# Up blocks of a gated FFN formed by token instead of by feature, and turned by DMA

## The chip, the cores and the metric

The kernel runs on one core of one Trainium2 chip. The metric is device time in microseconds of one execution, the median over runs. The engines are TensorE (PE; its weight loads are listed as PEld), VectorE (DVE), ScalarE (ACT), GpSimd (POOL) and SyncE (SP), whose queue issues nearly all DMAs here. SBUF is the memory that engines and DMAs work from; PSUM takes what TensorE forms.

## The reference

One decoder layer on 256 tokens of width 2048, in float32: retention and a gated linear recurrence side by side, a gated merge, attention over 256 memory tokens, a convolved gated FFN, and a last norm. The change is in the FFN:

```
def causal_dwconv(x, w, bias):
...
def conv_gated_ffn(hn, w_up, conv_w, conv_b, w_down):
    up = causal_dwconv(hn @ w_up, conv_w, conv_b)
    gate, val = jnp.split(up, 2, axis=-1)
    return (jax.nn.silu(gate) * val) @ w_down
...
    hn = rmsnorm(h, norm_ffn_w[l])
    h = h + conv_gated_ffn(hn, ffn_w_up[l], ffn_conv_w[l], ffn_conv_b[l], ffn_w_down[l])
    return rmsnorm(h, final_norm_w)
```

`w_up` is 2048 x 11264 (5632 gate features, then 5632 value features). The convolution has three taps over tokens, one set per feature. `w_down` is 5632 x 2048.

## The kernel before

All weights are streamed once from HBM, in one order fixed beforehand (`weight_plan`), in chunks of four k tiles: 4 x 128 rows of 512 columns, 1 MB. A block is 512 columns over all rows, so four chunks for 2048 rows. `prefetch` issues each chunk's load on SP's queue into one of three raw buffers and splits it in halves of two k tiles: `hi` is the weight rounded to the float32r that TensorE multiplies (L248, on ACT), `lo` the remainder (L249, on DVE). There are six buffers of each, three chunks' worth; two chunks are split ahead of the one in use. The activations are split the same way, in pairs of k tiles: a tile `s` holds hi in columns 0 to 255 (tokens) and lo in columns 256 to 511. Each product is formed as hi\*hi + hi\*lo + lo\*hi.

There are two forms of a block.

By feature (`gemm_t`, L309): 128x128 of the weights is held stationary, tokens stream. With `hi` held, one matmul of 512 columns multiplies both halves of `s`; with `lo` held, one of 256 multiplies the hi half. The result has features on partitions, in two accumulators of 128x2x512, each with two sums that have still to be added: `joined` copies one (L388, ACT) and adds the other (L389, DVE).

By token (`gemm_n`, L322 to L324): the activations are held stationary, 128 tokens of one k tile, and 512 weight columns stream; three matmuls for each k tile and each half of the tokens. The result has tokens on partitions, in one accumulator.

The norms' factor for each token is applied behind the product. In the by-feature form it varies along the free axis, so DVE multiplies by a copy spread over all partitions (`scaled`, L528). In the by-token form it is one number for each partition.

`by_dma` turns 256 tokens x 512 features around. ACT copies the two 16-bit halves of each float32 into two planes (L367); two DMA transposes on SP's queue, one for each half of the tokens, turn the planes (L369); one chunk later (`later(1, join)`) ACT puts the halves together again (L378) and hands the result on. It is used for the merge and for the two residuals, `residual` (L800 is the add, L815 the squares for the norm), whose results are needed by feature next.

The FFN runs in three parts of four, four and three pairs of blocks (`FF_PARTS`). A pair is a gate block and a value block of `w_up`, each by feature: `conv_up` takes the accumulators as they come, applies `scaled`, and does the convolution, one tap on ACT (L916) and two on DVE (L918). Then the gating: tanh on ACT (L985), two operations on DVE (L986, L987), and the split into `hid` (L399, L400). After a part's up blocks come its four down blocks, by token, with `hid` held stationary and the result added to the rows of the residual stream (`down`, L929). The last part's last down block also does the final norm.

The order of instructions on each engine is set by a scheduler that goes by the order in the program and by priorities; `tc.high_priority(URGENT)` moves a step ahead. Accumulators come from a pool of three, the large SBUF tiles (`big`) from a pool of 27.

Of the kernel before, what the change touches and what calls it, by code (L numbers as in the profile page):

```python
# [13 lines left out]
AF = mybir.ActivationFunctionType  # L14
ALU = mybir.AluOpType
AX = mybir.AxisListType

P = 128
D = 2048
S = 256  # L20
NT = D // P
# [5 lines left out]
FF = 5632  # L27
NF = FF // P
BW = 512
# [6 lines left out]
URGENT = 5  # L36
# [79 lines left out]
def hybrid_layer(  # L116
# [16 lines left out]
    act, dve, pe, pool, sp = nc.scalar, nc.vector, nc.tensor, nc.gpsimd, nc.sync  # L133
# [11 lines left out]
    def nm(s):  # L145
        count[0] += 1
        return f"{s}_{count[0]}"

    def big(shape, dt=F32, s="b"):
        return bp.tile(shape, dt, tag="big", name=nm(s))  # L150

    def tmp(s="t"):
        return tp.tile([P, 2, S], F32, tag="tmp", name=nm(s))
# [19 lines left out]
    pf = cp.tile([P, 4, NF2], F32, name="pf")  # L173
# [85 lines left out]
    def later(n, fn):  # L259

        pending.append((step[0] + n + 1, fn))
# [18 lines left out]
    def ended(steps):  # L280

        for a in steps:
            pass
        return a
# [31 lines left out]
    def gemm_t(*args):  # L316
        return ended(steps_t(*args))
# [8 lines left out]
    def steps_n(w, row, st, nk, col):  # L326

        a = acc()
        for k0, n, parts in chunks(nk, w, row, col):
            for tt in range(2):  # L330
                for kk in range(n):
                    k = k0 + kk
                    hi, lo = (t[:, kk % KH, :] for t in parts[kk // KH])
                    products_n(a[:, tt, :], st[k // 2][:, k % 2, :], hi, lo, tt, k == 0, k == nk - 1)
            yield a

    def gemm_n(*args):
        return ended(steps_n(*args))
# [21 lines left out]
    def by_dma(rows, then):  # L360


        planes = big([P, 2, 2, BW], U16, s="pl")
        turned_ = big([P, 2, 4, S], U16, s="pt")
        words = rows.bitcast(U16).rearrange("p t (n h) -> p h t n", h=2)
        for h in range(2):
            act.copy(planes[:, :, h, :], words[:, h])  # L367
        for tt in range(2):
            sp.dma_start_transpose(  # L369
                out=turned_.rearrange("p h f s -> p (h f) s")[:, :, tt * P : (tt + 1) * P],  # L370
                in_=planes[:, tt].rearrange("p h n -> p (h n)"),
            )

        def join():
            f = big([P, 4, S], s="f")
            halves_ = f.bitcast(U16).rearrange("p f (s h) -> p h f s", h=2)
            for h in range(2):
                act.copy(halves_[:, h], turned_[:, h])  # L378
            then(f)

        later(1, join)

    def joined(a, s="j"):

        c = tmp("c")
        o = tmp(s)
        with tc.high_priority(URGENT):
            act.copy(c, a[:, :, S:BW])  # L388
            dve.tensor_tensor(out=o, in0=a[:, :, 0:S], in1=c, op=ALU.add)  # L389
        return o  # L390

    def split_pair(src, scale=None):

        t = big([P, 2, BW], F32R, s="s")
        if scale is None:
            act.copy(t[:, :, 0:S], src)
            dve.tensor_tensor(out=t[:, :, S:BW], in0=src, in1=t[:, :, 0:S].bitcast(F32), op=ALU.subtract)
        else:
            act.mul(t[:, :, 0:S], src, scale)  # L399
            dve.scalar_tensor_tensor(  # L400
                out=t[:, :, S:BW], in0=src, scalar=scale, in1=t[:, :, 0:S].bitcast(F32),
                op0=ALU.mult, op1=ALU.subtract,
            )
        return t
# [32 lines left out]
    def p_cw(i, t):  # L437
        return pa[:, 16 + i * 16 + t : 17 + i * 16 + t]
# [32 lines left out]
    def rstd_rows(ss):  # L471

        var = sp_.tile([P, 2], F32, tag="var", name=nm("var"))
        dve.tensor_reduce(out=var, in_=ss, axis=AX.X, op=ALU.add)
        return rsqrt_small(var, 2, 1.0 / D, EPS)
# [50 lines left out]
    def scaled(a, s):  # L526
        z = joined(a, s)
        dve.tensor_tensor(out=z, in0=z, in1=rsb2, op=ALU.mult)  # L528
        return z
# [115 lines left out]
    for g in range(2):  # L645
        dec = big([P, 4, S], s="dec")
        vs, turned = [], []
        for b, o in enumerate((O_Q, O_K)):
            a = [joined(t, "q") for t in gemm_t("w_in", 0, xs, NT, o + g * BW)] if g + b else qjoin
            if b == 1:  # L650
                sp.dma_start(
                    out=dec,
# [10 lines left out]
        for b in range(2):  # L663
            a = gemm_n("w_in", 0, xs, NT, O_G + g * 1024 + b * BW)
            t = big([P, 2, BW], s="gate")
# [70 lines left out]
    for b in range(4):  # L736
# [4 lines left out]
        for pr, a in enumerate(gemm_t("w_in", 0, xs, NT, O_XR + b * BW)):  # L741
            z = scaled(a, "xz")
            for j in range(2):
                t = 4 * b + 2 * pr + j
                y = xr[:, 2 * pr + j, :]
                act.activation(y, z[:, j, :], AF.Identity, scale=p_cw(3, t), bias=p_cb(t))
                for s in range(1, 4):
                    dve.scalar_tensor_tensor(  # L748
                        out=y[:, s:S], in0=z[:, j, 0 : S - s], scalar=p_cw(3 - s, t), in1=y[:, s:S],
                        op0=ALU.mult, op1=ALU.add,  # L750
                    )
        gl = big([P, 4, S], s="gl")
        for pr, a in enumerate(gemm_t("w_in", 0, xs, NT, O_YR + b * BW)):
            y = scaled(a, "yz")
            y2, th = tmp("y2"), tmp("yt")
# [5 lines left out]
                out=gl[:, 2 * pr : 2 * pr + 2, :], in0=th, scalar=1.0, in1=y, op0=ALU.add, op1=ALU.mult  # L761
# [21 lines left out]
    for b in range(4):  # L783
        m = gated(O_GA, "w_proj_ret", ret, b, big([P, 2, BW], s="m"))
        dve.tensor_add(m, m, mb[b])
        by_dma(m, turn_merged)
# [6 lines left out]
    def residual(w, st, out, wcol, steps=None):  # L793

        ss = sums()
        for b in range(4):
            if steps:
                steps(b)
            h = hrow[b]
            dve.tensor_add(h, h, gemm_n(w, 0, st, NT, b * BW))  # L800
            squares(h, ss, b)
            by_dma(hrow[b], lambda f, b=b: turn(f, b, out, wcol))
        return ss
# [70 lines left out]
    for b in range(XH):  # L874
        ks = []
        for a in gemm_t("xa_w_k", 0, ms, NT, b * BW):
            z = joined(a, "kz")
# [26 lines left out]
    h2s = []  # L904
    ss2 = residual("xa_w_o", osp, h2s, p_ffn)
    rs2 = rstd_rows(ss2)
    later(1, spread_tokens(rs2))


    def conv_up(c0, b, dst):  # L910
        for pr, a in enumerate(gemm_t("ffn_w_up", 0, h2s, NT, c0 + b * BW)):
            z = scaled(a, "uz")
            for j in range(2):
                t = c0 // P + 4 * b + 2 * pr + j
                y = dst[:, 2 * pr + j, :]
                act.activation(y, z[:, j, :], AF.Identity, scale=pf[:, 2, t : t + 1], bias=pf[:, 3, t : t + 1])  # L916
                for s in range(1, 3):
                    dve.scalar_tensor_tensor(  # L918
                        out=y[:, s:S], in0=z[:, j, 0 : S - s], scalar=pf[:, 2 - s, t : t + 1], in1=y[:, s:S],
                        op0=ALU.mult, op1=ALU.add,  # L920
                    )

    def down(b0, hid, b, final):

# [49 lines left out]
    b0 = 0  # L974
    for part, nb_ in enumerate(FF_PARTS):
        final = part == len(FF_PARTS) - 1
        hid = []
        for b in range(b0, b0 + nb_):
            gt, vl = big([P, 4, S], s="fg"), big([P, 4, S], s="fv")
            conv_up(0, b, gt)  # L980
            conv_up(FF, b, vl)
            for pr in range(2):
                cs = slice(2 * pr, 2 * pr + 2)
                th, o = tmp("ft"), tmp("fo")
                act.activation(th, gt[:, cs, :], AF.Tanh, scale=0.5)  # L985
                dve.scalar_tensor_tensor(out=o, in0=th, scalar=1.0, in1=gt[:, cs, :], op0=ALU.add, op1=ALU.mult)  # L986
                dve.tensor_tensor(out=o, in0=o, in1=vl[:, cs, :], op=ALU.mult)  # L987
                hid.append(split_pair(o, 0.5))
        if final:
            wfin = []  # L990
            for i in range(2):
                t = big([P, 2, BW], s="wf")
                sp.dma_start(
                    out=t.rearrange("p a n -> p (a n)"),
                    in_=final_norm_w[i * 1024 : (i + 1) * 1024].partition_broadcast(P),
                )
                wfin.append(t)
        for b in range(4):
            down(b0, hid, b, final)
        b0 += nb_  # L1000
# [33 lines left out]
```

## Time and profile before

| | |
|---|---|
| median of 3 runs | 2039.36 us (2038.9 to 2040.87) |
| the profiled execution | 2038.96 us, its span 2037.2 |
| mean granted clock of TensorE | 0.999 |
| bytes read from HBM | 388.46 MB, 192 GB/s over the span |
| up and down blocks | from 1301 us to the end |
| DMA transposes | 24, from 708.7 to 1305.1 us |

Times in the profile are from the span's start. A group's mean is the time of one instruction of it; matmuls overlap each other, so their spacing, which the chain of waits shows, is shorter than their mean (391 ns for one of 512 columns). "Granted clock" is the share of full speed that the throttle allowed. In the stretches, each engine's busy time stands with the number of its instructions behind it.

Durations that the text uses:

| line | engine, what | count | mean ns |
|---|---|---|---|
| L248 | ACT, hi of a half chunk | 710 | 1049 |
| L249 | DVE, lo of a half chunk | 710 | 1223 |
| L388, L389 | ACT copy, DVE add out of PSUM, 128x512 | 84, 84 | 580, 688 |
| L528 | DVE, spread scale, 128x512 | 44 in the FFN | 688 |
| L916, L918 | ACT tap, DVE tap of the FFN's convolution | 88, 176 | 597, 478 |
| L985, L986, L987 | gating | 22 each | 623, 686, 687 |
| L399, L400 | split of the gated result | 22 each | 631, 688 |
| L367, L378 | ACT, plane copy, join copy | 24, 24 | 1038, 1350 |
| L412 | DVE, three operands, one in PSUM, 128x512 | 16 | 748 |
| L959 | DVE, scaling by a number for each partition in SBUF, 128x512 | 2 | 488 |

### The profile page before, as it was taken

How to read it: one execution, taken by the hardware profiler on the slowest of the kernel's cores; microseconds unless marked ns; L12 is line 12 of the kernel's file. 1: busy time of each engine (PE TensorE's matmuls, PEld its weight loads, DVE VectorE, ACT ScalarE, POOL GpSimd, SP SyncE). 2: the span in 40 equal slices, each digit the busy share in tenths (PEclk: the TensorE clock that was granted, in tenths of full speed). 3: DMA queues.
4: the chain of work that ended last, by engine and by line, in shares of the span. 5: the costliest groups of instructions: out<-in, count | busy, mean ns of one | idle time of the engine just before them, and what ended most of it. 6: DMA issues, size and time to landing. Idle time of an engine off the chain costs nothing.

```text
span 2037.2 us, 26091 instructions
## 1 busy us (share of the span) xinstructions
PE 2024.4 (99%) x10412; PEld 1736.3 (85%) x10412; DVE 1306.7 (64%) x1631; ACT 1091.1 (54%) x1406; POOL 7.7 (0%) x12
## 2 busy tenths in 40 slices
PE   9999999999999999999999999999999999999998
PEld 7888888888888888888888888888888888888887
DVE  6848658888444455466555555577764777646774
ACT  6545447677443455496444556655543555434553
POOL 0000000000000000000000000000000000000000
PEclk9999999999999999999999999999999999999999
DMA  8554554444555556776444446644544545554553
GB/s 318 225 198 162 199 187 163 181 176 170 214 194 186 197 202 217 257 254 238 168 184 181 171 166 198 216 186 189 199 192 186 191 181 198 195 187 185 195 217 105
DMA packets 90121, 398.53 MB, mean 196 GB/s; under 512 B 32400, under 2 KB 37136, under 8 KB 44944
## 3 DMA queue, kind: packets, MB, share of 16 engines
q1 hardware_dynamic: 88480, 394.25, 52.4%
q10 hardware_dynamic: 1520, 2.63, 0.4%
q8 instruction: 81, 1.33, 0.2%
q14 instruction: 40, 0.33, 0.0%
HBM read 388.46 MB, written 2.10 MB: 192 GB/s over the span
## 4 chain that ended last, share of the span: by engine, by line
PE 79%; ACT 0%; DVE 0%; issue 0%; POOLq 0%; DVEq 0%
PE acc L309 35%; PE acc L323 14%; PE acc L322 14%; PE acc L324 14%; PE sm L343 1%; PE sm L710 0%; ACT hi L248 0%; DVE xr L727 0%; PE sm L866 0%; ACT pl L367 0%; ACT nat L961 0%; DVE lo L249 0%; ACT c L388 0%; PE sm L455 0%; ACT s L399 0%
## 5 line engine op out<-in xcount | busy, mean ns | idle before, releaser
L249 DVE TENSOR_TENSOR lo<-raw,hi 128x1024 fp32r<-128x1024 f32 (+1 forms) x714 | 858.1, 1220 | 603.6 <-ACT hi L248 562.9
L248 ACT CAST hi<-raw 128x1024 fp32r<-128x1024 f32 (+1 forms) x712 | 732.4, 1048 | 670.7 <-PE acc L323 401.6
L309 PE MATMUL acc<-s,hi 128*128 128x512 f32 x2688 | 637.1, 391 | 0.6 <-ACT c L388 0.4
L322 PE MATMUL acc<-hi,s 128*128 128x512 f32 (+1 forms) x1528 | 590.1, 386 | 1.6 <-ACT hi L248 1.6
L323 PE MATMUL acc<-hi,s 128*128 128x512 f32 (+1 forms) x1528 | 589.9, 386 | 0.0
L324 PE MATMUL acc<-lo,s 128*128 128x512 f32 (+1 forms) x1528 | 589.8, 386 | 0.0
L309 PEld LDWEIGHTS acc<-s,hi 128*128 128x128 f32 x2688 | 496.5, 188 | 99.8 <-ACT hi L248 0.8
L309 PEld LDWEIGHTS acc<-s,lo 128*128 128x128 f32 x2688 | 342.2, 191 | 13.8 <-DVE lo L249 1.7
L309 PE MATMUL acc<-s,lo 128*128 128x256 f32 x2688 | 350.0, 284 | 1.6 <-ACT s L422 1.0
L322 PEld LDWEIGHTS acc<-hi,s 128*128 128x128 f32 x1528 | 287.1, 188 | 59.3 <-ACT hi L248 2.1
L324 PEld LDWEIGHTS acc<-lo,s 128*128 128x128 f32 x1528 | 287.0, 188 | 58.5 <-DVE lo L249 0.7
L323 PEld LDWEIGHTS acc<-hi,s 128*128 128x128 f32 x1528 | 287.1, 188 | 57.1 <-DVE s L400 0.4
L388 ACT COPY c<-acc 128x512 f32<-128x512 f32 x84 | 48.5, 580 | 107.1 <-PE acc L309 107.1
L389 DVE TENSOR_TENSOR uz<-acc,c 128x512 f32<-128x512 f32 x44 | 30.3, 688 | 26.6 <-ACT c L388 26.6
L918 DVE SCALAR_TENSOR_TENSOR fg<-uz,pf,fg 128x255 f32<-128x255 f32 (+1 forms) x88 | 39.0, 478 | 0.0
L918 DVE SCALAR_TENSOR_TENSOR fv<-uz,pf,fv 128x255 f32<-128x255 f32 (+1 forms) x88 | 38.4, 478 | 0.0
L378 ACT COPY f<-pt 128x1024 uint16<-128x1024 uint16 x24 | 30.8, 1350 | 10.2 <-DMA pt<-pl 10.1
L528 DVE TENSOR_TENSOR uz<-uz,rsb 128x512 f32<-128x512 f32 x44 | 30.3, 688 | 0.7
L399 ACT ACTIVATE s<-fo 128x512 fp32r<-128x512 f32 x22 | 13.9, 631 | 26.6 <-DVE fo L987 26.6
L916 ACT ACTIVATE fv<-uz,pf 128x256 f32<-128x256 f32 x44 | 25.2, 597 | 2.5 <-DVE uz L528 2.5
L916 ACT ACTIVATE fg<-uz,pf 128x256 f32<-128x256 f32 x44 | 25.2, 596 | 0.0
L748 DVE SCALAR_TENSOR_TENSOR xr<-xz,pa,xr 128x255 f32<-128x255 f32 (+2 forms) x48 | 20.0, 480 | 0.0
(167 smaller groups left out, 748.3 us busy)
## 6 DMA issues: line engine op xcount, KB each, us to landing
raw<-in_wall SPq DMA_DIRECT2D x352, 1024.0 KB, 4.8
raw<-in_wall SPq DMA_DIRECT2D x6, 512.0 KB, 6.1
nat<-in_x ACTq DMA_DIRECT2D x4, 512.0 KB, 8.3
nat<-in_x SPq DMA_DIRECT2D x4, 512.0 KB, 5.8
nat<-in_mem SPq DMA_DIRECT2D x4, 512.0 KB, 8.9
xt<-in_mem_t SPq DMA_DIRECT2D x8, 256.0 KB, 5.9
xt<-in_x_t SPq DMA_DIRECT2D x7, 256.0 KB, 7.3
out<-nat SPq DMA_DIRECT2D x6, 256.0 KB, 2.8
```

The source lines that it names most:

```text
L248: act.copy(hi[:, ds], raw[:, cs, :])
L249: dve.tensor_tensor(out=lo[:, ds], in0=raw[:, cs, :], in1=hi[:, ds].bitcast(F32), op=ALU.subtract)
L309: pe.matmul(a, part, sx, start=k == 0 and t == 0, stop=k == nk - 1 and t == 0, skip_group_check=True)
L322: pe.matmul(o, h, hi, start=start, stop=False)
L323: pe.matmul(o, l, hi, start=False, stop=False)
L324: pe.matmul(o, h, lo, start=False, stop=stop)
L378: act.copy(halves_[:, h], turned_[:, h])
L388: act.copy(c, a[:, :, S:BW])
L389: dve.tensor_tensor(out=o, in0=a[:, :, 0:S], in1=c, op=ALU.add)
L528: dve.tensor_tensor(out=z, in0=z, in1=rsb2, op=ALU.mult)
L916: act.activation(y, z[:, j, :], AF.Identity, scale=pf[:, 2, t : t + 1], bias=pf[:, 3, t : t + 1])
L918: dve.scalar_tensor_tensor(out=y[:, s:S], in0=z[:, j, 0 : S - s], scalar=pf[:, 2 - s, t : t + 1], in1=y[:, s:S], op0=ALU.mult, op1=ALU.add,)
```

## The change

All gate blocks, and all value blocks but the last of each part, are formed by token with `gemm_n`: 7, 7 and 5 of 22. Their accumulator is scaled by DVE on its way out of PSUM into a tile `rows` (`turned_rows`), at raised priority, and handed to `by_dma`. The convolution then runs on the turned block, one chunk into the next block, and the gating after the value block's. The last value block of each part is as before (`conv_up_t`). The arithmetic of the convolution and the gating is the same; their code moves into functions.

```diff
+    def turned_rows(a, r, then):
+
+        rows = big([P, 2, BW], s="rows")
+        with tc.high_priority(URGENT):
+            for tt in range(2):
+                if r is None:
+                    dve.tensor_copy(rows[:, tt, :], a[:, tt, :])
+                else:
+                    dve.tensor_scalar_mul(rows[:, tt, :], a[:, tt, :], r[:, tt : tt + 1])
+        by_dma(rows, then)
...
-    def conv_up(c0, b, dst):
+    def conv(z, t0, dst):
+
+        for j in range(z.shape[1]):
+            t = t0 + j
+            y = dst[:, j, :]
+            act.activation(y, z[:, j, :], AF.Identity, scale=pf[:, 2, t : t + 1], bias=pf[:, 3, t : t + 1])
+            for s in range(1, 3):
+                dve.scalar_tensor_tensor(
+                    out=y[:, s:S], in0=z[:, j, 0 : S - s], scalar=pf[:, 2 - s, t : t + 1], in1=y[:, s:S],
+                    op0=ALU.mult, op1=ALU.add,
+                )
+
+    def conv_up(c0, b, dst, then):
+
+
+        def turned(f):
+            conv(f, c0 // P + 4 * b, dst)
+            then()
+
+        turned_rows(gemm_n("ffn_w_up", 0, h2s, NT, c0 + b * BW), rs2, turned)
+
+    def conv_up_t(c0, b, dst):
+
         for pr, a in enumerate(gemm_t("ffn_w_up", 0, h2s, NT, c0 + b * BW)):
-            z = scaled(a, "uz")
...
+            conv(scaled(a, "uz"), c0 // P + 4 * b + 2 * pr, dst[:, 2 * pr : 2 * pr + 2, :])
...
             gt, vl = big([P, 4, S], s="fg"), big([P, 4, S], s="fv")
-            conv_up(0, b, gt)
-            conv_up(FF, b, vl)
...
+            conv_up(0, b, gt, lambda: None)
+            if b < b0 + nb_ - 1:
+                conv_up(FF, b, vl, lambda gt=gt, vl=vl: gate_up(gt, vl, hid))
+            else:
+                conv_up_t(FF, b, vl)
+                gate_up(gt, vl, hid)
```

`gate_up` is the gating of before as a function: for each of two pairs of feature tiles, tanh, two operations on DVE, and the split that is appended to `hid`.

More of the change, by code (lines that the diff above doesn't have):

```diff
@@ L907, in hybrid_layer, with gate_up @@
     later(1, spread_tokens(rs2))
-    def conv_up(c0, b, dst):
-        for pr, a in enumerate(gemm_t("ffn_w_up", 0, h2s, NT, c0 + b * BW)):
-            z = scaled(a, "uz")
[L913 to L921, printed above, removed]
+    def conv(z, t0, dst):
[14 more added lines that the diff above has]
+    def conv_up_t(c0, b, dst):
+        for pr, a in enumerate(gemm_t("ffn_w_up", 0, h2s, NT, c0 + b * BW)):
+            conv(scaled(a, "uz"), c0 // P + 4 * b + 2 * pr, dst[:, 2 * pr : 2 * pr + 2, :])
+    def gate_up(gt, vl, hid):
+        for pr in range(2):
+            cs = slice(2 * pr, 2 * pr + 2)
+            th, o = tmp("ft"), tmp("fo")
+            act.activation(th, gt[:, cs, :], AF.Tanh, scale=0.5)
+            dve.scalar_tensor_tensor(out=o, in0=th, scalar=1.0, in1=gt[:, cs, :], op0=ALU.add, op1=ALU.mult)
+            dve.tensor_tensor(out=o, in0=o, in1=vl[:, cs, :], op=ALU.mult)
+            hid.append(split_pair(o, 0.5))
     def down(b0, hid, b, final):
@@ L979, in hybrid_layer @@
             gt, vl = big([P, 4, S], s="fg"), big([P, 4, S], s="fv")
-            conv_up(0, b, gt)
-            conv_up(FF, b, vl)
[L982 to L988, printed above, removed]
+            conv_up(0, b, gt, lambda: None)
[4 more added lines that the diff above has]
+                gate_up(gt, vl, hid)
         if final:
```

## The prediction

> **What bounds the kernel now.** I read the page first, then the waits of TensorE alone, then the chain of work that ended last, cut to the FFN, then stretches of single blocks and the timeline of one block end.
>
> ```profile
> PE 2024.4 (99%) x10412; PEld 1736.3 (85%) x10412; DVE 1306.7 (64%) x1631; ACT 1091.1 (54%) x1406; POOL 7.7 (0%) x12
> ```
>
> TensorE is busy 2024.4 of 2037.2 us. Its waits say how little is left to fill:
>
> ```profile
> PE acc L322 <- ACT hi L248: 1.6, 1, 1.6
> PE warm L188 <- DVE mhalf L183: 1.1, 1, 1.1
> PE acc L309 <- ACT s L422: 1.0, 1, 1.0
> ```
>
> So a block of weights gains only by costing less on TensorE itself, and loses by starving it. The chain in the FFN gives the cost of both forms of a block of 2048x512 weights (columns: start us, us, what):
>
> ```profile
> 1564.17 177.95 PE acc L309 x1024
> 1742.11 0.23 PE acc L322
> ...
> 1829.18 133.45 PE acc L309 x768
> ```
>
> The first line is the second part's eight up blocks by feature: 1024 matmuls, 177.95 us without a gap, 22.244 us a block (the last line: 133.45/6 = 22.242). Between 1742.11 and 1829.18 lie that part's four down blocks by token: 87.07 us, 21.767 us a block. Both forms stream the same 49152 columns a block: by feature 64 matmuls of 512 and 64 of 256, by token 96 of 512. What differs is the number of matmuls, 128 against 96.
>
> **The change part by part.** *TensorE.* In each FFN part all up blocks but the last value block go by token: 7 + 7 + 5 = 19. 19 x (22.244 - 21.767) = 19 x 0.477 = **-9.1 us**. In terms of one matmul: 87.07/384 = 0.2267 us for 512 columns, and (22.244 - 64 x 0.2267)/64 = 0.1208 us for 256, which is a fixed 15 ns beside 0.414 ns a column; 32 matmuls fewer x 15 ns = 0.48.
>
> The Trainium skill (TensorE: Matmul & The Clock Gate, "Back-to-back issue gap") gives a warm gap of columns/2.4 + 2.5 ns, so a fixed cost of only 2.5 ns a matmul; an estimate by that page is 19 x 32 x 2.5 ns = 1.5 us of gain, not 9. The trace does not agree: 226.7 ns where the page has 215.8 for 512 columns, and 15 ns fixed. The measurement decides for the sum; that no difference between the forms survives in the up stage is a rival below.
>
> *DVE.* Per block it loses two adds of the halves (L389, 688 ns) and two multiplications by the spread scale (L528, 688 ns), 2.75 us. It gains two scalings of 128x512 out of PSUM, an operation the trace does not show. Bounds: 0.49 us (L959, a scaling of that size in SBUF) and 0.75 us (L412, three operands, one of them PSUM). I take 0.69, as L389 reads PSUM in 0.688: 1.4 us. The convolution (L918, eight of 0.478 us) and the gating (L986, L987, L400) move, and cost the same. Mean per block, with eight splits L249 of 1.22: 18.5 us of 22.24 before, 17.1 of 21.77 after (78%; 76 to 79 by the bounds).
>
> *ACT.* It loses two copies of 580 ns (L388), and gains two plane copies (L367, 1.04 us) and two joins (L378, 1.35 us): +3.6 us a block. With eight casts L248 of 1.05, four L916 of 0.60 and half of the gating (2.5/2): 13.2 us before, 16.8 after (77%).
>
> *DMA and SP's queue.* Two more transposes a block, 38 in all, beside 24 now. The stage that already runs this way, by token, with two transposes and two joins in each block, is the residual after attention (L800). Four stretches, the third and fourth of one block each:
>
> ```profile
> core 0: us, PE busy (x) PEld busy (x) DVE busy (x) ACT busy (x) POOL busy (x), PEclk, DMA share, GB/s
> 850.00:900.00 50.00, 50.00 (x224) 41.47 (x223) 28.97 (x35) 40.56 (x63) 0.70 (x1) 1.00 0.80 283
> 1390.00:1440.00 50.00, 50.00 (x297) 44.58 (x296) 39.27 (x58) 28.57 (x39) 0.00 (x0) 1.00 0.45 173
> 1238.65:1260.40 21.75, 21.75 (x97) 18.02 (x96) 12.17 (x13) 15.26 (x21) 0.00 (x0) 1.00 0.74 215
> 1260.40:1282.20 21.80, 21.80 (x98) 18.03 (x97) 12.16 (x13) 15.22 (x21) 0.00 (x0) 1.00 0.65 214
> ```
>
> TensorE has no idle time in any. So the transposes take the DMA engines from about 0.50 to 0.65-0.74 and fit; ACT at 81% (first row) fits; DVE at 79% (second row) fits. What no row shows is DVE at 78% and ACT at 77% together. So look at how late things may be. One block end there:
>
> ```profile
> 1255.84 1.22 DVE L800 TENSOR_TENSOR nat<-nat,acc 128x1024 f32<-128x1024 f32 x1
> 1258.33 1.98 ACT L367 COPY pl<-nat 128x1024 uint16<-128x1024 uint16 x2
> 1260.33 2.98 SPq L369 DMA_TRANSPOSE pt<-pl  x2
> 1263.68 16.62 SPq L223 DMA_DIRECT2D raw<-in_wall  x4
> 1265.49 2.57 ACT L378 COPY f<-pt 128x1024 uint16<-128x1024 uint16 x2
> 1275.36 1.05 ACT L248 CAST hi<-raw 128x1024 fp32r<-128x1024 f32 x1 [2.90 <-PE acc L323]
> ```
>
> The block ends at 1255.84 (the add was waiting for it). The planes are done 4.5 us later, the transposes hold SP's queue until 7.8 us, and the next weights are issued only then; the joins start after 9.7 us. Yet at 19.5 us ACT waits 2.90 us for TensorE to free a split buffer: it is as far ahead as the buffers let it be. The next add follows at 1277.59, 21.75 us after the first.
>
> In the changed kernel, by its instruction order as built, three waits are added at the same places. The scaling waits on DVE for the block's end; behind it stands the second half of the split of the third chunk ahead, which TensorE reaches after two chunks, 10.9 us (21.77/2). The planes wait on ACT for 1.4 us of scaling, without the squares of L815 that the residual has in between, so they are done about 3.5 us after the end, 1 us earlier than above. The transposes wait on SP behind three to five weight loads, with the next load behind them; they are through at 3.5 + 3.0 = 6.5 us instead of 7.8, and a load lands in 4.8. The joins wait on ACT for the transposes, behind the first cast of the fifth chunk ahead or so, which itself waits for buffers; the chunk that they delay is due two chunks later. The convolution takes 2.4 us of ACT behind the joins, where this stage has the four scalings L422 (1.7 us) and after them 2.90 us idle, and 3.8 us of DVE, which here stands idle for 2 to 3 us several times a block. I charge **0**, with a bound of one shortage per block (the rival below) on the dear side; no gain is possible, as these blocks have no idle time now.
>
> *Ends of the parts.* The last value block of each part stays by feature, so its results reach the down blocks as now; its gate block turns behind it and is joined one chunk into it. The first up block needs the last pair of the residual's output at its fourth chunk in both forms. Charged 0; if the cover went, the nearest shortage is the 1.03 us that TensorE waited at 925.5, at the end of the other residual.
>
> **Sum.** The profiled execution took 2038.96 us, 2037.2 of it span. 2038.96 - 9.1 = 2029.9; the median of the runs, 2039.36, is 0.4 above it: **2030.3 us**, 0.44% less.
>
> **The rivals.**
>
> *B, slower: splits come late.* ACT and DVE work in series (L249 waits for L248, 562.9 us in all) and are now both near four fifths; if transposes land late, ACT stands still in its join, the casts behind it slip, and TensorE waits at each block. For it: TensorE's wait of 1.03 us at 925.5, where ACT had been 83% busy (24.87 of 30 us in 900 to 930), and the queue held for 3 us a block. Against: the four blocks of the residual without idle time, and ACT waiting for TensorE there. At 1.03 us a block, 19 x 1.03 = 19.6: 2030.3 + 19.6 = 2049.9 us. It decides from 0.477 us a block on, where the gain is gone.
>
> *C, no gain on TensorE.* The 0.477 us belongs to the stages and not to the form, so that 96 matmuls in the up stage cost what 128 do. For it: the page's rule named above, and that both forms have as many columns. Against: by token the block takes 21.75 us in the attention residual and 21.77 in the down stage, by feature 22.25 at 986.18 (33.37 us for 192 matmuls of the attention), other stages with other loads. Time: 2039.4 less 0 to 1.5, say 2038.6 us.
>
> *D, only the seams lose.* The three parts each begin with a first block after another stage and end in a block by feature behind a turned one; at 1.03 us each, 6 x 1.03 = 6.2: 2036.5 us. For it: the one recorded shortage sits at such a seam. Against: the seam at 1301 into the first up block shows none.
>
> **How the numbers follow.** The forecast 0.74, B 0.13, C 0.06, D 0.07. What a measurement here can tell from no change is 0.2%, 4.1 us: 2035.3 to 2043.4 is "same". Faster 0.76: the forecast, and 0.02 of D at half its price or less; same 0.11: the rest of D and C; slower 0.13: B. Range: 2028.0 (the scaling cheaper is of no use to TensorE, so only rounding in the 0.477 and the spread of runs lie below) to 2038.0, which takes in D and leaves out B and most of C, under 0.2. The forecast's own range is 2028 to 2034.
>
> **What would show it.** In the changed profile: a chain in the FFN of L322 to L324, with blocks of 21.77 us; L309 down to 2688 - 19 x 64 = 1472 of each form; TensorE's waits still some us in all; 62 transposes; the scaling at about 0.69 us; ACT's casts still waiting for TensorE in the up stage. Wrong would be: TensorE waiting for L248 or L249 in the up stage by more than 0.2 us a block (B), or blocks of 22.2 us without waits (C).

## The result and the profile after

| | median us | range | runs |
|---|---|---|---|
| before | 2039.89 | 2038.49 to 2042.3 | 20 |
| changed | 2036.74 | 2032.68 to 2041.44 | 20 |

The ratio is 0.9985, with a 95% interval of 0.9979 to 0.9991: faster by 3.2 us. That is inside the stated range of 2028 to 2038, but only a third of the 9.1 us forecast, and outside the likeliest case's own range of 2028 to 2034. By the prediction's own division (2035.3 to 2043.4 is "same") it lies in the outcome that was given 0.11; the interval over 20 runs of each kernel is narrower than the 0.2% that was assumed, and leaves out no change. The changed kernel's runs also spread over 8.8 us where those before spread over 3.8. Its profiled execution lies near the upper end of this spread: 2040.3 us, span 2038.5.

From the page of the changed kernel (busy time, then idle before the group and what ended it):

```profile
PE 2021.6 (99%) x9804; PEld 1709.8 (84%) x9804; DVE 1282.4 (63%) x1593; ACT 1154.0 (57%) x1444; POOL 7.7 (0%) x12
...
L378 ACT COPY f<-pt 128x1024 uint16<-128x1024 uint16 x62 | 79.4, 1347 | 59.1 <-DMA pt<-pl 59.0
L367 ACT COPY pl<-rows 128x1024 uint16<-128x1024 uint16 x38 | 37.9, 1044 | 47.5 <-DVE rows L391 47.5
...
L391 DVE TENSOR_SCALAR rows<-acc,ro 128x512 f32<-128x512 f32 x38 | 26.7, 744 | 0.0
```

The same group of joins on the page of the kernel before:

```profile
L378 ACT COPY f<-pt 128x1024 uint16<-128x1024 uint16 x24 | 30.8, 1350 | 10.2 <-DMA pt<-pl 10.1
```

The 62 transposes are there, and the scaling takes 0.744 us. New is how long ACT stands idle in the new steps: 59 us in front of the joins L378, waiting for a transpose to land, where the kernel before had 10, and 47.5 us in front of the plane copies. The waits of TensorE in the changed kernel (us in all, number, longest):

```profile
PE acc L309 <- DVE lo L249: 3.5, 2, 1.8
PE acc L323 <- DVE s L411: 1.7, 1, 1.7
PE acc L322 <- ACT hi L248: 1.3, 1, 1.3
```

Before there were under 5 us in all, none in the up stage. Now one of the two waits of the first line (1.83 us, at 1460.6) is in the last value block of the first part, the block by feature; the second line's 1.7 us is at the end of the last part, where the down block needs the last gated result. The rest of these three lines is at the start. These two waits cost more than themselves. Stretches of the changed kernel (us, busy times, TensorE's granted clock after POOL):

```profile
1461.50:1462.00 0.50, 0.00 (x0) 0.00 (x0) 0.50 (x1) 0.00 (x0) 0.00 (x0) 1.00 0.00 0
...
1464.00:1465.00 1.00, 1.00 (x5) 0.96 (x5) 1.00 (x2) 1.00 (x2) 0.00 (x0) 0.50 0.89 360
1465.00:1466.00 1.00, 1.00 (x4) 0.75 (x3) 0.93 (x1) 1.00 (x2) 0.00 (x0) 0.50 1.02 434
...
1467.00:1467.50 0.50, 0.50 (x3) 0.41 (x3) 0.50 (x1) 0.50 (x1) 0.00 (x0) 1.00 1.10 215
```

TensorE goes on at 1462.4, and 1.2 us later its clock is granted at half, from about 1463.6 to 1467: some 3.4 us that do the work of 1.7. So 1.83 us of waiting cost about 3.5. The wait of 1.71 us that ended at 1975.0 is followed by the same, from 1975.6 on. The shorter one of 1.03 us in the kernel before (at 925.5) was not. Length alone does not decide it, as the last section shows.

DVE's adds onto the residual rows mark the same points in each kernel (their starts in the timelines). Part 1 is measured from the last add of the attention residual to its first down add, the others from the fourth down add of the part before to their second:

| us | before | forecast | changed | e1_pin3 | e2_noturn |
|---|---|---|---|---|---|
| up to the FFN | 1299.35 | the same | 1302.37 | 1298.12 | 1300.96 |
| part 1 (7 blocks changed) | 200.26 | 196.92 | 200.80 | 196.85 | 196.85 |
| part 2 (7) | 221.49 | 218.15 | 218.36 | 218.10 | 218.08 |
| part 3 (5) | 166.48 | 164.09 | 167.55 | 164.61 | 164.06 |

The changed kernel gained what was forecast in part 2, and lost 3.9 and 3.5 us against the forecast in the two parts that have a wait near their end. Another 3.0 us of the profiled execution lie before the FFN, where the instructions are those of before: over the profiled executions of this study that mark falls between 1298.12 and 1302.37. All of it arises at the start of the program. There the changed kernel's clock stands at 0.50 from about 19.8 to 26.6 us, and TensorE works for 5.9 us of that time, which costs about 3.0; the profiled execution of before shows no fall there. At 29 us the changed kernel is 3.55 us behind the one before, at the FFN 3.0. Which execution has such a fall varies: e2_noturn has one too (from 21 to 24.5 us), e1_pin3 has none.

### The profile page after: what moved, and what is told of

Read it like the earlier page. It is cut to its first block, busy times and chain, and to the rows that moved or that the text cites. A ratio compares the mean times of both kernels' runs of the same rounds, so it can differ in the third digit from the quotient of the medians.

```text
span 2038.5 us, 24966 instructions
## 1 busy us (share of the span) xinstructions
PE 2021.6 (99%) x9804; PEld 1709.8 (84%) x9804; DVE 1282.4 (63%) x1593; ACT 1154.0 (57%) x1444; POOL 7.7 (0%) x12
## 3 DMA queue, kind: packets, MB, share of 16 engines
q8 instruction: 76, 1.25, 0.2%
## 4 chain that ended last, share of the span: by engine, by line
PE 77%; DVE 1%; ACT 1%; issue 0%; DMA 0%; POOLq 0%; SPq 0%; DVEq 0%; ACTq 0%
PE acc L323 21%; PE acc L324 20%; PE acc L322 20%; PE acc L309 14%; PE sm L343 1%; DVE lo L249 1%; PE sm L721 0%; ACT hi L248 0%; DMA pt<-pl 0%; DVE fv L928 0%; DVE fg L928 0%; DVE s L411 0%; ACT f L378 0%; ACT pl L367 0%; DVE xr L738 0%
## 5 line engine op out<-in xcount | busy, mean ns | idle before, releaser
L249 DVE TENSOR_TENSOR lo<-raw,hi 128x1024 fp32r<-128x1024 f32 (+1 forms) x714 | 858.7, 1219 | 642.0 <-ACT hi L248 612.2
L248 ACT CAST hi<-raw 128x1024 fp32r<-128x1024 f32 (+1 forms) x712 | 731.6, 1048 | 587.1 <-PE acc L323 437.3
L322 PE MATMUL acc<-hi,s 128*128 128x512 f32 (+1 forms) x2136 | 827.8, 388 | 1.3 <-ACT hi L248 1.3
L323 PE MATMUL acc<-hi,s 128*128 128x512 f32 (+1 forms) x2136 | 827.4, 387 | 1.7 <-DVE s L411 1.7
L324 PE MATMUL acc<-lo,s 128*128 128x512 f32 (+1 forms) x2136 | 826.8, 387 | 0.0
L323 PEld LDWEIGHTS acc<-hi,s 128*128 128x128 f32 x2136 | 401.8, 188 | 82.8 <-DVE s L411 2.2
L322 PEld LDWEIGHTS acc<-hi,s 128*128 128x128 f32 x2136 | 401.6, 188 | 82.8 <-ACT hi L248 1.5
L324 PEld LDWEIGHTS acc<-lo,s 128*128 128x128 f32 x2136 | 401.5, 188 | 82.1 <-DVE lo L249 0.4
L309 PE MATMUL acc<-s,hi 128*128 128x512 f32 x1472 | 353.1, 393 | 0.6 <-ACT c L399 0.4
L309 PEld LDWEIGHTS acc<-s,hi 128*128 128x128 f32 x1472 | 274.0, 190 | 56.1 <-issue 0.5
L309 PE MATMUL acc<-s,lo 128*128 128x256 f32 x1472 | 197.3, 286 | 4.5 <-DVE lo L249 3.5
L309 PEld LDWEIGHTS acc<-s,lo 128*128 128x128 f32 x1472 | 190.7, 193 | 12.6 <-DVE lo L249 4.9
L378 ACT COPY f<-pt 128x1024 uint16<-128x1024 uint16 x62 | 79.4, 1347 | 59.1 <-DMA pt<-pl 59.0
L367 ACT COPY pl<-rows 128x1024 uint16<-128x1024 uint16 x38 | 37.9, 1044 | 47.5 <-DVE rows L391 47.5
L410 ACT ACTIVATE s<-fo 128x512 fp32r<-128x512 f32 x22 | 13.7, 632 | 12.8 <-DVE fo L953 12.8
```

The lines of the kernel that those rows point to most:

```text
L248: act.copy(hi[:, ds], raw[:, cs, :])
L249: dve.tensor_tensor(out=lo[:, ds], in0=raw[:, cs, :], in1=hi[:, ds].bitcast(F32), op=ALU.subtract)
L309: pe.matmul(a, part, sx, start=k == 0 and t == 0, stop=k == nk - 1 and t == 0, skip_group_check=True)
L322: pe.matmul(o, h, hi, start=start, stop=False)
L323: pe.matmul(o, l, hi, start=False, stop=False)
L324: pe.matmul(o, h, lo, start=False, stop=stop)
```

## The experiments

Theory T: ACT takes its queue in order. Where the join stands in front of casts and its transpose has not landed, ACT waits although the weights behind it lie ready. The splits lose some of their lead over the blocks, and by the end of a part TensorE waits. Rival L: ACT and DVE simply have too much to do in series. Rival S: at the seam, where a block by feature follows blocks by token, TensorE stalls whatever the engines' lag.

The lag can be read from the changed kernel's timeline of DVE: the scalings of the first part (start us, us). TensorE's blocks are 21.76 us apart; the starts are not:

```profile
1324.62 1.40 DVE L391 TENSOR_SCALAR rows<-acc,ro 128x512 f32<-128x512 f32 x2
1348.77 1.41 DVE L391 TENSOR_SCALAR rows<-acc,ro 128x512 f32<-128x512 f32 x2
...
1414.62 1.41 DVE L391 TENSOR_SCALAR rows<-acc,ro 128x512 f32<-128x512 f32 x2
1437.89 1.40 DVE L391 TENSOR_SCALAR rows<-acc,ro 128x512 f32<-128x512 f32 x2
1462.26 1.40 DVE L391 TENSOR_SCALAR rows<-acc,ro 128x512 f32<-128x512 f32 x2
```

Six blocks are 130.6 us, and 1324.62 + 130.6 = 1455.2: the last scaling is 7 us late. The lag grows in steps: counted the same way it is 2.4 us in the second block, 3.0 in the fifth, 4.5 in the sixth and 7.1 in the seventh. In part 2, where TensorE waits for nothing, the seventh is 4.1 us late (1590.16 to 1724.80). One block of the changed kernel shows how that comes about (ACT's timeline; in brackets the idle time before and what ended it):

```profile
1416.07 2.00 ACT L367 COPY pl<-rows 128x1024 uint16<-128x1024 uint16 x2 [2.27 <-DVE rows L391]
1417.97 2.00 ACT L248 CAST hi<-raw 128x1024 fp32r<-128x1024 f32 x2
1424.35 2.55 ACT L378 COPY f<-pt 128x1024 uint16<-128x1024 uint16 x2 [4.38 <-DMA pt<-pl]
1426.77 1.04 ACT L248 CAST hi<-raw 128x1024 fp32r<-128x1024 f32 x1
```

Two casts, then 4.38 us of standing for the transpose, and DVE, whose next split needs the cast at 1426.77, stands with it for 6.43 us. The casts behind the join wait for nothing when they come: six of them run between 1426.77 and 1435.7, while TensorE takes 2.72 us (21.76/8) to use up one half chunk. So there was work ready behind the join.

**The join further back (e1_pin2, e1_pin3).** The join is due one or two chunks later, and its copies are held to the program's order. Nothing is taken out.

```diff
-    def by_dma(rows, then):
+    def by_dma(rows, then, wait=1):
...
-                act.copy(halves_[:, h], turned_[:, h])
+                i = act.copy(halves_[:, h], turned_[:, h])
+                if wait > 1:
+                    tc.keep_in_program_order(i)
...
-        later(1, join)
+        later(wait, join)
...
-        by_dma(rows, then)
+        by_dma(rows, then, 3)
```

(with 2 in place of 3 in e1_pin2; the last line is the one in `turned_rows`)

> The join of a turned up block is put two casts further back on ScalarE (behind the splits of the fourth chunk after the two that were ready), nothing else. Theory T (ScalarE stands in the join for the transposes, 59 us in all, while casts are queued behind it; the lead of the splits wears away over a part and TensorE waits in the part's last value block): the 59 us of waits for transposes fall below 20, the scalings L391 no longer slip from 0.5 to 7.5 us behind the block's end, TensorE waits for no split in the FFN, time 2031 to 2033. Rival L (ScalarE and VectorE, near four fifths busy each and in series, are simply too slow): no change, 2036 to 2038. Rival S (a block by feature behind blocks by token stalls in any case): no change, 2036 to 2038.

> The same with the join another chunk later. T: waits for transposes gone altogether, time 2031 to 2033, unless the results of the last pair come too late for the down blocks, which would show as TensorE waiting for the split L411 or its line here at the three part ends and cost 2 to 4 us each. L and S: 2036 to 2038 or more.

e1_pin2: 2031.06 us (2030.33 to 2031.56), ratio 0.9956 (0.9942 to 0.9969). e1_pin3: 2030.69 (2028.98 to 2031.72), 0.9954 (0.9941 to 0.9966). The waits of e1_pin3, all engines (us in all, number, longest):

```profile
ACT hi L248 <- PE acc L323: 519.9, 354, 4.8
...
ACT f L378 <- DMA pt<-pl: 7.3, 6, 1.9
```

The same view of e1_pin3, TensorE alone:

```profile
PE acc L322 <- ACT hi L248: 1.3, 1, 1.3
...
PE acc L323 <- DVE s L413: 0.4, 1, 0.4
```

In e1_pin3 ACT waits 7.3 us for transposes instead of 59 (19.1 in e1_pin2), and waits longer for TensorE to free split buffers, 519.9 us instead of 437.3: it is ahead again. In the trace of e1_pin2 the joins stand behind four casts, counted from the plane copies of their block, in e1_pin3 behind four to six; in the changed kernel it was two or three. ACT's wait before the plane copies shrinks too, from 47.5 us to 13.0 in e1_pin3. Within the FFN alone (from 1303 us on) ACT waits 51.4 us for transposes in the changed kernel, 11.9 in e1_pin2 and none in e1_pin3; the 7.3 us left are in the merge and the residuals. TensorE's waits are down to those before the FFN and 0.4 us at the end of the last part, and the whole 9.1 us of gain is there (2039.75 - 2030.69 = 9.06). T holds, and L and S fall, for the engines' work and the seams are as they were. That the transposes hold up the weights on SP's queue is not the cause either: in the FFN ACT waits 6.1 us for weights in the changed kernel and 6.1 us in e1_pin3. Not all that was expected came: in e1_pin3 the scalings still start up to 6 us late in every other block (1412.65 and 1456.16 in part 1, but not 1429.60). The lateness does not grow, and TensorE doesn't feel it.

**No transposes (e2_noturn).** The up blocks' transposes are left out, so the FFN works on blocks that are not turned. The copies stay.

```diff
-        for tt in range(2):
+        for tt in range(2 if turn_ else 0):
...
-            halves_ = f.bitcast(U16).rearrange("p f (s h) -> p h f s", h=2)
+            if turn_:
+                halves_ = f.bitcast(U16).rearrange("p f (s h) -> p h f s", h=2)
+            else:
+                halves_ = f.rearrange("p f s -> p (f s)").bitcast(U16).rearrange("p (t n h) -> p h t n", t=2, h=2)
...
-                act.copy(halves_[:, h], turned_[:, h])
+                act.copy(halves_[:, h], turned_[:, h] if turn_ else planes[:, :, h, :])
```

> The transposes of the 19 up blocks are left out, the join reads the planes directly, so the FFN works on blocks that are not turned; the plane copies and the joins stay. T: ScalarE no longer waits for DMA, TensorE does not wait in the FFN, the full gain of 19 x 0.477 = 9.1 us, 2030.8 (2030 to 2032). L and S: the engines' work is the same, 2036 to 2038.

2029.94 us (2029.73 to 2031.3), ratio 0.9952 (0.994 to 0.9965). The scalings of part 1 now stand at even distances:

```profile
1323.20 1.40 DVE L394 TENSOR_SCALAR rows<-acc,ro 128x512 f32<-128x512 f32 x2
1344.96 1.40 DVE L394 TENSOR_SCALAR rows<-acc,ro 128x512 f32<-128x512 f32 x2
...
1453.76 1.40 DVE L394 TENSOR_SCALAR rows<-acc,ro 128x512 f32<-128x512 f32 x2
```

(1453.76 - 1323.20)/6 = 21.76 us, the cost of a block by token in the up stage. The same 160 us of the first part, of the changed kernel and of this one:

```profile
1300.00:1460.00 160.00, 160.00 (x716) 132.71 (x714) 104.45 (x141) 108.35 (x130) 0.70 (x1) 1.00 0.65 207
```

```profile
1300.00:1460.00 160.00, 160.00 (x723) 133.11 (x722) 113.22 (x149) 115.45 (x135) 0.70 (x1) 1.00 0.56 197
```

TensorE is full in both. DVE and ACT are *less* busy in the slower kernel, 104.45 and 108.35 us against 113.22 and 115.45: most of the difference is work that it has not done yet (its FFN also begins 1.4 us later). A mean load of 71 and 72%, which e2_noturn carries without a wait of TensorE in the FFN, was not the limit.

**The last pair by feature (e3_lastpair, e8_lastpair_pin3).** The last gate block of each part goes by feature too; 16 blocks change. The second kernel has the joins of e1_pin3 as well.

```diff
-            conv_up(0, b, gt, lambda: None)
             if b < b0 + nb_ - 1:
+                conv_up(0, b, gt, lambda: None)
...
             else:
+                conv_up_t(0, b, gt)
                 conv_up_t(FF, b, vl)
```

> The last gate block of each part is formed by feature too, 16 blocks by token: full gain 16 x 0.477 = 7.6, so 2032.3 without stalls. T: one block less to slip and no turned block behind the seam; stalls mostly gone, 2032 to 2034. L: likewise, a little less slip, 2033 to 2036. S: the seam between the forms is there as before, 2036.7 + 1.4 = 2038.

> Joins three chunks back, and the last gate block of each part by feature as well: 16 blocks by token, full gain 7.6, 2032.3. T: with the splits and the evictions on time, two blocks by feature in a row cost nothing more, as in the kernel before: 2032 to 2034. If the two blocks by feature behind a turned one stall for want of an accumulator whatever the engines' lag: 2045 to 2051 as in the run without the later joins.

e3_lastpair: 2050.42 us (2049.65 to 2052.15), ratio 1.0053 (1.0041 to 1.0066), slower than before and far from what any theory had expected. Its waits of TensorE begin with

```profile
PE acc L309 <- DVE uz L400: 12.5, 3, 6.3
```

once in each part. Two blocks by feature need four accumulators, and the pool has three; the fourth is free when DVE has added up the first (L400). DVE was as late as in the changed kernel (the sixth scaling of part 1 starts 5.1 us behind the block's end, 5.0 there), so TensorE waited for it. With the joins further back the same two blocks cost nothing: e8_lastpair_pin3 took 2033.24 us (2032.26 to 2034.36), 0.9971 (0.9959 to 0.9982), within a microsecond of the 2032.3 that 16 blocks give. So the seam is where the lag is paid and not its cause: S falls a second time.

**One copy only (e7_join2).** As e1_pin2, but without the lines that hold the copies to the program's order.

> The join due one chunk later in the program's order but left to the scheduler, which puts it only one cast further back on ScalarE (between the two casts of the fourth chunk). T: between the changed kernel and the one with the join two casts back: waits for transposes 20 to 45 us, 2032 to 2036.

2049.99 us (2049.36 to 2051.09), 1.0055 (1.0041 to 1.0069), far above what T had expected. In the trace the first of the two join copies mostly stands behind three casts, counted from the plane copies of its block, as most joins do in the changed kernel (the others behind two), and one cast stands between it and the second. ACT stood 64.1 us for transposes, no less than in the changed kernel, and the join was finished later; TensorE waited 11.5 us for splits and gated results in the FFN. So the step at which the program asks for the join does not settle its place in ACT's queue. How much of the 13 us over the changed kernel comes from the joins is not shown: the gating steps moved as well, and ACT waited 23.3 us for gated results instead of 12.8.

**Transposes twice (e5_twice, e6_twice_pin3).** Each up block's two transposes are issued a second time behind the first, into the same tile: in the changed kernel, and in e1_pin3.

```diff
-        for tt in range(2):
+        for tt in (0, 1, 0, 1) if twice else (0, 1):
```

> The changed kernel with each up block's transposes issued twice, the second pair writing the same tile again behind the first. T: ScalarE stands in each join some 3 to 5 us longer, 19 times; the lead of the splits is used up earlier in each part, TensorE waits in the middle of a part; time above 2045, up to 2039.9 + 19 x 3 = 2097. If a late transpose did not matter (L or S): at most a few us above 2036.7.

> The same doubling in the kernel whose joins are three chunks back. T: the second pair lands before the join is reached; ScalarE waits little, 2031 to 2035. If it is the transposes' load on the DMA engines or the hold-up of the weight loads behind them on SP's queue that made the changed kernel slow, doubling it costs here as in the other: above 2040, with casts waiting for weights.

e5_twice: 2080.49 us (2077.98 to 2082.93), 1.0202 (1.0188 to 1.0216), 43.8 over the changed kernel, with 118.8 us of ACT standing in the joins and TensorE waiting 32.6 us in all for L249, L248, L410 and L411, mostly within the parts. e6_twice_pin3: 2054.37 (2051.63 to 2059.34), 1.0077 (1.0064 to 1.0089), 23.7 over e1_pin3, which T had not expected. This is the outcome that had been tied to the other explanation, weight loads held up on SP's queue. Its waits show both effects at once: joins waiting again (52.8 us), and casts waiting for weights, since the second pair holds SP's queue (3.5 to 7.8 us each time) with weight loads behind it:

```profile
ACT hi L248 <- DMA raw<-in_wall: 57.1, 24, 6.7
ACT f L378 <- DMA pt<-pl: 52.8, 14, 9.5
```

In e1_pin3 these are 24.4 and 7.3. So the hold-up of the weights is real when the transposes are doubled; with the transposes as they are, e1_pin3 has the whole gain. Later joins take away the cost of the transposes as they are; they do not make transposes free.

**All kernels side by side.** The scheduler lays out ACT's queue anew for each kernel, so none differs from the changed one by its one edit alone: in e2_noturn the first join copy mostly stands behind one cast, in e5_twice behind four or five, and in e1_pin2 and e1_pin3 gating steps moved by a place or two. What goes with the loss in all of them is how long ACT stands in the joins of the FFN, though not in proportion. The loss is counted from the full gain, 9.1 us (7.6 for the two kernels with 16 blocks) below the kernel before in the same set of runs; the upper four lie within the spread of the runs:

| kernel | ACT waiting for transposes in the FFN, us | loss against the full gain, us |
|---|---|---|
| e2_noturn | 0 | -0.7 |
| e1_pin3 | 0 | 0.0 |
| e8_lastpair_pin3 | 0 | 1.4 |
| e1_pin2 | 11.9 | 0.4 |
| e3_lastpair | 44.5 | 18.3 |
| e6_twice_pin3 | 45.7 | 24.1 |
| changed | 51.4 | 6.0 |
| e7_join2 | 56.6 | 19.7 |
| e5_twice | 112.5 | 50.2 |

## Why the prediction was wrong

*Right.* A block by token costs 21.76 us in the up stage (forecast 21.77), so rival C is out. With ACT no longer standing, the three parts gain 3.41, 3.41 and 2.42 us in e2_noturn, and 3.34, 3.34 and 2.39 were forecast: the -9.1 us of TensorE is right to 0.2. The scaling was put at 0.69 us and took 0.744, within its bounds. The planes were done 3.5 us after the scaling began, as forecast. The Trainium skill (TensorE: Matmul & The Clock Gate, "Back-to-back issue gap") gives the 2.5 ns for one matmul by itself, and says that in a stream weight loads and matmuls set the spacing together. The estimate of 1.5 us in all that was made from the 2.5 ns does not agree with the 9.2 us that the three parts gained.

*Wrong: the step "I charge 0" for the splits.* It rested on one block end of the attention residual and asked whether a chunk delayed in that block would still be in time, two chunks later. It would, and TensorE has no wait in the first blocks. But the wait for the transposes comes again in each block, and what ACT and DVE do not catch up within 21.76 us is carried into the next: 7 us of lag after seven blocks. In place of 0 the profiled execution paid 3.9 us at the end of part 1 and 3.5 at the end of part 3. The residual has four blocks and DVE busy 12.2 of 21.8 us, so it did not show it. The mechanism is that of rival B (casts slip behind a join), with a price for each part instead of each block, at the ends of parts, where rival D had put it. The prediction's own sign for B, over 0.2 us of waiting for splits in each block, would have missed it: 1.83 us over 19 blocks are 0.1.

*Wrong in size: the transposes.* The text took SP's queue to be held for 3.0 us, and the transposes to be through 6.5 us after the block's end. In the up stage of the changed kernel SP was held 2.6 to 6.0 us for a pair, and the median landing of a transpose rose from 3.7 to 4.4 us. The 3.0 us came from one row; the twelve pairs of the kernel before already range from 2.6 to 4.6. Two small readings were off without bearing on the sum: by the durations given, DVE's work before adds up to 18.4 us a block (18.5 in the text), and in the row shown the transposes held the queue until 7.5 us after the block's end (7.8 is when the next load was issued).

*Missing: the clock.* In the profiled execution the stalls of 1.71 and 1.83 us each cost about twice their length, and no term of the sum had a place for it.

*Rival D.* Its 2036.5 us lie next to the measured 2036.74, which is in part luck: it charged six ends with 1.03 us each, and the profiled execution pays some 3.5 to 4 us at two of them. Which ends are hit in the other nineteen runs can't be seen, since only the profiled execution has a trace; that they differ in it is only the likely reading of the spread of 8.8 us, which shrinks to 2.7 in e1_pin3 (five runs instead of twenty). The mean granted clock of each run fits it: 0.998 or 0.999 in the eight runs under 2036 us, 0.995 to 0.998 in the twelve above; falls at the start of the program count in it too.

## What to carry to other kernels

On an engine that takes its queue in order, a step that waits for a DMA belongs behind the work that is ready, and it has to be looked up in the built order whether it is there. A small delay in each block that a deep buffer hides is not free: count it over all blocks until something resets the lead, and expect the bill at the step that needs the most at once. Here a changed order of ACT's queue turned 3.2 us of gain into 9.1, and e1_pin3 (2030.69 us) and e1_pin2 (2031.06), whose ranges overlap, are the fastest complete versions.

## What the hardware showed that was not expected

TensorE's granted clock fell to 0.50 for some 3.4 us, 1.2 and 0.5 us after waits of 1.83 and 1.71 us had ended in the changed kernel's FFN. But no length of wait separates those that are followed by a fall from those that are not. Near 20 us, at the same first wait for a split, the kernel before waited 1.56 us and its clock stayed at 1.00, while e8_lastpair_pin3 waited 1.25 us and its clock fell to 0.50 from about 20.6 to 24.0. In e6_twice_pin3 two waits of 2.20 and 2.26 us (up to 1757.07 and 1760.99) and in e3_lastpair one of 3.01 us (up to 1952.38) left it at 1.00. What decides it is open. Two transposes of one block, issued together, held SP's queue between 2.6 and 6.0 us in the same kernel.
